# The sums of squares of an RMS norm, added over the partitions as two exact parts in fp32r products

## The chip, the cores and the metric

The kernel runs on one core of one Trainium2 chip. The metric is the device time of one launch in microseconds, taken as the median of three runs. A core has a matrix engine (PE, which loads a stationary operand and streams a moving one through it, the result landing in PSUM), a vector engine (DVE), a scalar engine (ACT), GpSimd (POOL) and SyncE (SP, which here issues nearly all the loads). Each engine takes its own instructions strictly in the order in which they were written into the program; between engines they wait for semaphores.

## The reference

A decoder trunk of two layers on 512 tokens of 1024 features, all in float32. Each sub-layer is wrapped in two RMS norms, and it is these norms that the change touches:

```python
def rms_norm(x, g):
    xf = x.astype(jnp.float32)
    y = xf * lax.rsqrt(jnp.mean(xf * xf, axis=-1, keepdims=True) + EPS)
    return (y * g.astype(jnp.float32)).astype(x.dtype)

f = swiglu(rms_norm(x, g[0]), w_ffn_gate[layer, 0], w_ffn_up[layer, 0], w_ffn_down[layer, 0])
x = x + 0.5 * rms_norm(f, g[1])
h = rms_norm(x, g[2])
# layer 0: m = short_conv_mixer(h, ...); layer 1: m = diff_attention(h, k, v, ...)
x = x + rms_norm(m, g[3])
f = swiglu(rms_norm(x, g[4]), ...)
x = x + 0.5 * rms_norm(f, g[5])
```

There are six sub-layers in a row: FFN, convolution, FFN (layer 0), FFN, attention, FFN (layer 1). So there are five boundaries between sub-layers, and at each of them the post-norm of one sub-layer is followed by the pre-norm of the next.

## The kernel before

Features lie on the 128 partitions (eight tiles `k` of 128), tokens on the free axis. Every large product is made in float32 accuracy from fp32r products: an operand is split into a rounded part `hi` (a cast, on ACT) and the exact rest `lo` (a subtraction, on DVE), and three products hi·hi, hi·lo and lo·hi are accumulated in one PSUM bank (`products`, lines 141 to 147). Weights come in units of 128x1024 over SP's queue into one of two `raw` buffers, and are split by a cast on ACT (`whi`, line 126) and a subtraction on DVE (`wlo`, line 127); seven split units are kept.

At a boundary (`closing`, line 254) the tokens are taken in two halves of 256 columns. `rms(t)` finishes the last tiles of the sub-layer's result `f` for one half, adds up the squares of its eight tiles in two accumulators (`facc0`, `facc1`, even and odd tiles, on DVE, line 190), and `total_of` (line 192) adds those up over the partitions: a PE product with the constant matrix `halves[D]` (all entries -0.5/1024), whose result `tot` stands in PSUM. `inv_rms` (line 169) turns it into 1/rms: ACT `n_y` (line 176), ACT `n_q` (line 178), DVE `n_q` (line 179), DVE `r` (line 180). `post` then scales `f`, adds it to the residual `x` and makes the `h_hi` and `h_lo` of the next sub-layer. The sequence is:

1. `rms(one)`, then `post` of the first half;
2. `rms(two)`, while the first half's `h` is made;
3. the head of the next sub-layer for the first half: PE products of `h` into PSUM banks `acc`;
4. `rest(one)`: squares of the new `x` of the first half, in `xacc0` and `xacc1`, their total, and the pre-norm factor `r2`;
5. the head's gate, which reads the `acc` banks, scales them by `r2` (lines 408 and 410; in the convolution lines 506 to 513) and so sets the banks free for the next PE products; `post` of the second half runs in between;
6. `rest(two)`.

There are six PSUM banks for such sums, and two small ones for `tot`.

Before the change `total_of` has two forms. With `merge` (the first half of `rms` and the second half of `rest`) DVE adds the two accumulators and one float32 product follows; without it (second half of `rms`, first half of `rest`) two float32 products are accumulated. There are 22 totals: ten in `rms` and twelve in `rest` (two of these before the first sub-layer), 11 of each form.

The order of the work on each engine isn't written out by hand. A scheduler decides it from its own costs when the program is built, so an edit in one helper can move other instructions.

Of the kernel before, what the change touches and what calls it, by code (L numbers as in the profile page):

```python
# [10 lines left out]
F32R = mybir.dt.float32r  # L11
BF16 = mybir.dt.bfloat16
AF = mybir.ActivationFunctionType
ALU = mybir.AluOpType
# [3 lines left out]
P = 128  # L18
D = 1024
S = 512  # L20
# [16 lines left out]
TEMPS = 4  # L37
HALF_TEMPS = 6
RAW = 2
WARM = 9  # L40
LAMBDA_INIT = 0.8 - 0.6 * math.exp(-0.3 * 1)
MASKED = -3.0e38
# [3 lines left out]
def yoco_kernel(ctx: ExitStack, tc, i, out):  # L46
    nc = tc.nc

    const = ctx.enter_context(tc.tile_pool(name="const", bufs=1))
    xpool = ctx.enter_context(tc.tile_pool(name="xpool", bufs=1))  # L50
    apool = ctx.enter_context(tc.tile_pool(name="apool", bufs=5 * NK))
    wsp = ctx.enter_context(tc.tile_pool(name="wsp", bufs=WUNITS))
    wraw = ctx.enter_context(tc.tile_pool(name="wraw", bufs=RAW))
    mpool = ctx.enter_context(tc.tile_pool(name="mpool", bufs=1))
    tpool = ctx.enter_context(tc.tile_pool(name="tpool", bufs=1))
    small = ctx.enter_context(tc.tile_pool(name="small", bufs=4))
    rpool = ctx.enter_context(tc.tile_pool(name="rpool", bufs=1))

    def slot(dtype, name):
        return apool.tile([P, S], dtype, tag="a", name=name)  # L60
# [7 lines left out]
    def temp(n=S, name="t"):  # L68
        if n <= S // 2:
            return tpool.tile([P, S // 2], F32, tag="th", name=name, bufs=HALF_TEMPS)[:, :n]  # L70
        return tpool.tile([P, S], F32, tag="t", name=name, bufs=TEMPS)[:, :n]
# [9 lines left out]
    halves = {}  # L81
    for n in (D, 2 * HD):
        halves[n] = const.tile([P, P], F32, name=f"half{n}")
        nc.vector.memset(halves[n], -0.5 / n)
    eps = const.tile([P, 1], F32, name="eps")
    nc.vector.memset(eps, EPS)
    gn = const.tile([P, 12, NK], F32, name="gn")
# [20 lines left out]
    warm = pst.tile([P, S], F32, tag="st", name="warm")  # L108
    for _ in range(WARM):
        nc.tensor.matmul(warm[:, :P], halves[D], halves[D], start=True, stop=True)  # L110
# [23 lines left out]
    def split(dst_hi, dst_lo, src, on_act=True):  # L134
        if on_act:
            nc.scalar.copy(dst_hi, src)  # L136
        else:
            nc.vector.tensor_copy(dst_hi, src)
        nc.vector.tensor_tensor(dst_lo, src, dst_hi.bitcast(F32), op=ALU.subtract)  # L139
# [29 lines left out]
    def inv_rms(total, dst, n, by_log=False):  # L169

        y = temp(n, "n_y")
        if by_log:
            nc.scalar.activation(y, total, AF.Ln, bias=eps, scale=-2.0)
            nc.scalar.activation(y, y, AF.Exp, scale=-0.5)
        else:
            nc.scalar.activation(y, total, AF.Abs_reciprocal_sqrt, bias=eps, scale=-2.0)
        q = temp(n, "n_q")
        nc.scalar.square(q, y)
        nc.vector.scalar_tensor_tensor(q, total, -0.5 * EPS, q, op0=ALU.add, op1=ALU.mult)
        nc.vector.scalar_tensor_tensor(dst, q, 1.5, y, op0=ALU.add, op1=ALU.mult)  # L180

    def squares_of(accs, src, m):

        acc = accs[m % 2]
        if m < 2:
            nc.scalar.square(acc, src)
        else:
            sq = temp(src.shape[-1], "sq")
            nc.scalar.square(sq, src)
            nc.vector.tensor_tensor(acc, acc, sq, op=ALU.add)  # L190

    def total_of(accs, n, merge):
        tot = pst.tile([P, S], F32, tag="st", name="tot")[:, :n]
        if merge:
            nc.vector.tensor_tensor(accs[1], accs[0], accs[1], op=ALU.add)
            nc.tensor.matmul(tot, halves[D], accs[1], start=True, stop=True)
            return tot
        for j, acc in enumerate(accs):
            nc.tensor.matmul(tot, halves[D], acc, start=j == 0, stop=j == 1)
        return tot  # L200

    def new_h():
# [2 lines left out]
    class Prenorm:  # L205
# [22 lines left out]
        def rest(self, t):  # L228
            a, b = t
            accs = [rpool.tile([P, S // 2], F32, tag=z, name=z) for z in ("xacc0", "xacc1")]  # L230
            for k in range(NK):
                squares_of(accs, x[:, k, a:b], k)
            inv_rms(total_of(accs, b - a, a > 0), self.r2[:, a:b], b - a)

    def post(f, r1, c, t, after, ks=range(NK)):

        a, b = t
        for k in ks:
            d = temp(b - a, "d")
            nc.vector.scalar_tensor_tensor(d, f[k][:, a:b], c[:, k : k + 1], r1, op0=ALU.mult, op1=ALU.mult)  # L240
            nc.vector.tensor_tensor(x[:, k, a:b], x[:, k, a:b], d, op=ALU.add)  # L241
            after.hi(k, t)
            if k > 0:
                after.lo(k - 1, t)
        if k == NK - 1:
            after.lo(k, t)
# [3 lines left out]
    def run(steps):  # L250
        for _ in steps:
            pass

    def closing(groups, c, after, then, step=2):

        f = [slot(F32, "f") if p is None else p for p in groups.parts]
        faccs = [rpool.tile([P, S], F32, tag=z, name=z) for z in ("facc0", "facc1")]

        def finish(ms, t):
            a, b = t
            for m, acc in zip(ms, groups(ms, t)):
                if groups.parts[m] is None:
                    nc.scalar.copy(f[m][:, a:b], acc)
                else:
                    nc.vector.tensor_tensor(f[m][:, a:b], f[m][:, a:b], acc, op=ALU.add)
                squares_of([z[:, a:b] for z in faccs], f[m][:, a:b], m)

        def rms(t):  # L270
            a, b = t
            for m in range(NK - TAIL, NK):
                finish([m], t)
            r1 = temp(b - a, "r1")
            inv_rms(total_of([z[:, a:b] for z in faccs], b - a, a == 0), r1, b - a)
            return r1

        for m in range(0, NK - TAIL, step):
            finish(range(m, m + step), FULL)
        one, two = HALVES  # L280
        post(f, rms(one), c, one, after)
        r1 = rms(two)
        ahead = then(one)
        next(ahead, None)
        after.rest(one)
        post(f, r1, c, two, after, range(POST_FIRST))
        next(ahead, None)
        post(f, r1, c, two, after, range(POST_FIRST, NK))
        run(ahead)
        after.rest(two)  # L290
        run(then(two))
# [548 lines left out]
```

## Time and profile before

| what | value |
| --- | --- |
| three runs, median (lowest to highest) | 1916.57 us (1916.27 to 1917.65) |
| the profiled execution's own time | 1915.81 us |
| its span, from the first to the last instruction | 1914.1 us |
| mean granted PE clock | 0.999 |
| PE, DVE and ACT busy | 99%, 52%, 39% of the span |

In the listings a PE product of 256 columns takes 0.28 us from start to end, but the next one starts after 0.11 to 0.12 us; what a product costs is read from start to start. A float32 product shows as two records.

### The profile page before, as it was taken

What the parts mean: (1) busy time and instruction counts of PE and PEld (TensorE: products, weight loads), DVE (VectorE), ACT (ScalarE), POOL (GpSimd) and SP (SyncE); (2) the same over time, 40 slices, a digit from 0 to 9 for tenths busy, and PEclk for the clock granted to TensorE, in tenths of its full rate; (3) what the DMA queues carried; (4) which work ended last, traced back from release to release, by engine and by line L of the source; (5) the groups of instructions that cost most, each with busy time, mean ns of one, the idle gap of its engine ahead of it and who ended that gap; (6) DMA issues with size and microseconds to landing.
All of it is one profiled execution on the core that took longest, in us unless ns stands there. A gap on an engine that the chain in (4) does not pass through costs nothing.

```text
span 1914.1 us, 24278 instructions
## 1 busy us (share of the span) xinstructions
PE 1896.1 (99%) x9780; PEld 1601.2 (84%) x9780; DVE 993.0 (52%) x1671; ACT 738.8 (39%) x1248; POOL 1.1 (0%) x8
## 2 busy tenths in 40 slices
PE   9999999999999999999999999999999999999998
PEld 8888888988898888888988888899866898888886
DVE  7423434574566334344862443457389594234345
ACT  7322222453354322222633222335289673332132
POOL 0000000000000000000000000000000000000000
PEclk9999999999999999999999999999999999999999
DMA  4432323233323323332233332323211224233331
GB/s 168 120 101 91 106 88 102 74 94 94 112 76 104 106 87 101 91 108 89 66 114 100 103 100 95 90 87 94 72 34 59 74 67 132 78 99 100 98 89 65
DMA packets 53375, 178.45 MB, mean 93 GB/s; under 512 B 6288, under 2 KB 9488, under 8 KB 53264
## 3 DMA queue, kind: packets, MB, share of 16 engines
q1 hardware_dynamic: 52400, 175.94, 29.5%
q8 instruction: 77, 1.26, 0.3%
q10 hardware_dynamic: 864, 0.97, 0.2%
q14 instruction: 34, 0.28, 0.1%
HBM read 174.79 MB, written 2.10 MB: 92 GB/s over the span
## 4 chain that ended last, share of the span: by engine, by line
PE 87%; DVE 8%; ACT 3%; issue 1%; DMA 1%; SPq 0%; DVEq 0%; ACTq 0%
PE acc L146 25%; PE acc L147 25%; PE acc L145 25%; PE d_acc L358 2%; PE d_acc L356 2%; PE d_acc L357 2%; DVE d L240 1%; DVE h_lo L219 1%; DVE x L241 1%; DVE wlo L127 1%; PE v_acc L604 1%; PE v_acc L605 1%; PE v_acc L606 1%; ACT e L647 1%; DVE top L642 1%
## 5 line engine op out<-in xcount | busy, mean ns | idle before, releaser
L145 PE MATMUL acc<-h_hi,whi 128*128 128x512 f32 (+1 forms) x1952 | 696.3, 358 | 2.3 <-ACT whi L126 1.5
L146 PE MATMUL acc<-h_lo,whi 128*128 128x512 f32 (+1 forms) x1952 | 696.3, 357 | 0.2
L147 PE MATMUL acc<-h_hi,wlo 128*128 128x512 f32 (+1 forms) x1952 | 695.4, 357 | 0.8 <-DVE wlo L127 0.8
L126 ACT CAST whi<-raw 128x1024 fp32r<-128x1024 f32 (+2 forms) x336 | 334.5, 1019 | 869.3 <-PE acc L146 731.1
L127 DVE TENSOR_TENSOR wlo<-raw,whi 128x1024 fp32r<-128x1024 f32 (+2 forms) x336 | 396.5, 1182 | 237.8 <-ACT whi L126 236.7
L145 PEld LDWEIGHTS acc<-h_hi,whi 128*128 128x128 f32 x1952 | 366.4, 188 | 57.5 <-ACT whi L126 2.0
L147 PEld LDWEIGHTS acc<-h_hi,wlo 128*128 128x128 f32 x1952 | 366.7, 188 | 55.2 <-DVE wlo L127 1.0
L146 PEld LDWEIGHTS acc<-h_lo,whi 128*128 128x128 f32 x1952 | 367.3, 188 | 54.4 <-DVE h_lo L219 0.8
L408 DVE TENSOR_TENSOR gs<-acc,r 128x512 f32<-128x512 f32 (+1 forms) x100 | 62.6, 626 | 446.9 <-PE acc L147 446.7
L146 PE MATMUL acc<-act_lo,whi 128*128 128x512 f32 (+1 forms) x624 | 223.3, 358 | 0.0
L145 PE MATMUL acc<-act_hi,whi 128*128 128x512 f32 (+1 forms) x624 | 222.7, 357 | 0.0
L147 PE MATMUL acc<-act_hi,wlo 128*128 128x512 f32 (+1 forms) x624 | 222.7, 357 | 0.0
L146 PEld LDWEIGHTS acc<-act_lo,whi 128*128 128x128 f32 x624 | 117.6, 189 | 18.4
L145 PEld LDWEIGHTS acc<-act_hi,whi 128*128 128x128 f32 x624 | 117.2, 188 | 18.0
L147 PEld LDWEIGHTS acc<-act_hi,wlo 128*128 128x128 f32 x624 | 117.2, 188 | 17.8
L136 ACT CAST act_hi<-us 128x512 fp32r<-128x512 f32 (+1 forms) x100 | 56.5, 568 | 64.2 <-DVE us L412 64.2
L356 PE MATMUL d_acc<-whi,act_hi 128*128 128x512 f32 x176 | 68.4, 389 | 0.0
L357 PE MATMUL d_acc<-whi,act_lo 128*128 128x512 f32 x176 | 68.3, 389 | 0.0
L358 PE MATMUL d_acc<-wlo,act_hi 128*128 128x512 f32 x176 | 68.3, 389 | 0.0
L410 DVE TENSOR_TENSOR us<-acc,r 128x512 f32<-128x512 f32 (+1 forms) x100 | 62.6, 626 | 0.0
L139 DVE TENSOR_TENSOR act_lo<-us,act_hi 128x512 fp32r<-128x512 f32 (+1 forms) x100 | 61.8, 621 | 0.7 <-ACT act_hi L136 0.7
L412 DVE TENSOR_TENSOR us<-us,gs 128x512 f32<-128x512 f32 (+1 forms) x100 | 61.7, 621 | 0.3
(156 smaller groups left out, 1647.6 us busy)
## 6 DMA issues: line engine op xcount, KB each, us to landing
raw<-in_wg SPq DMA_DIRECT2D x85, 512.0 KB, 3.7
raw<-in_wu SPq DMA_DIRECT2D x85, 512.0 KB, 3.4
raw<-in_wd SPq DMA_DIRECT2D x48, 448.0 KB, 3.4
raw<-in_wd SPq DMA_DIRECT2D x24, 512.0 KB, 3.8
raw<-in_wci SPq DMA_DIRECT2D x24, 512.0 KB, 3.5
raw<-in_wdt SPq DMA_DIRECT2D x22, 512.0 KB, 3.7
raw<-in_wco SPq DMA_DIRECT2D x8, 512.0 KB, 3.6
raw<-in_wq SPq DMA_DIRECT2D x8, 512.0 KB, 3.5
```

The costliest lines, as they stand in the source:

```text
L126: nc.scalar.copy(hi[:, z], raw[:, z])
L127: nc.vector.tensor_tensor(lo[:, z], raw[:, z], hi.bitcast(F32)[:, z], op=ALU.subtract)
L139: nc.vector.tensor_tensor(dst_lo, src, dst_hi.bitcast(F32), op=ALU.subtract)
L145: nc.tensor.matmul(acc, wh, ah, start=first and j == 0, stop=False)
L146: nc.tensor.matmul(acc, wh, al, start=False, stop=False)
L147: nc.tensor.matmul(acc, wl, ah, start=False, stop=last and j == n - 1)
L356: nc.tensor.matmul(acc, ah, wh, start=k == 0, stop=False)
L357: nc.tensor.matmul(acc, al, wh, start=False, stop=False)
L358: nc.tensor.matmul(acc, ah, wl, start=False, stop=k == m1 - m0 - 1)
L408: nc.vector.tensor_tensor(gs, g, r2[:, p:q], op=ALU.mult)
L410: nc.vector.tensor_tensor(us, up, r2[:, p:q], op=ALU.mult)
L412: nc.vector.tensor_tensor(us, us, gs, op=ALU.mult)
```

## The change

`total_of` loses its `merge` argument. Both accumulators are now split like any other operand, into `acc_hi` (ACT cast) and `acc_lo` (DVE subtraction), and four fp32r products with an fp32r copy of the constant matrix, `half_r`, are accumulated. The four new tiles and `half_r` need room, and the space reserved for descriptors of software-made DMA is set to 512 bytes; no DMA of the kernel is issued from POOL.

```diff
+SCRATCH = 512
...
+    half_r = const.tile([P, P], F32R, name="half_r")
+    nc.vector.tensor_copy(half_r, halves[D])
...
-    def total_of(accs, n, merge):
+    def total_of(accs, n):
+
         tot = pst.tile([P, S], F32, tag="st", name="tot")[:, :n]
-        if merge:
-            nc.vector.tensor_tensor(accs[1], accs[0], accs[1], op=ALU.add)
-            nc.tensor.matmul(tot, halves[D], accs[1], start=True, stop=True)
-            return tot
         for j, acc in enumerate(accs):
-            nc.tensor.matmul(tot, halves[D], acc, start=j == 0, stop=j == 1)
+            hi, lo = (rpool.tile([P, S // 2], F32R, tag=f"acc{z}{j}", name=f"acc_{z}")[:, :n] for z in ("hi", "lo"))
+            split(hi, lo, acc)
+            nc.tensor.matmul(tot, half_r, hi, start=j == 0, stop=False)
+            nc.tensor.matmul(tot, half_r, lo, start=False, stop=j == 1)
         return tot
...
-            inv_rms(total_of(accs, b - a, a > 0), self.r2[:, a:b], b - a)
+            inv_rms(total_of(accs, b - a), self.r2[:, a:b], b - a)
...
-            inv_rms(total_of([z[:, a:b] for z in faccs], b - a, a == 0), r1, b - a)
+            inv_rms(total_of([z[:, a:b] for z in faccs], b - a), r1, b - a)
...
-    nc = bacc.Bacc("TRN2", target_bir_lowering=False, num_devices=1)
+    nc = bacc.Bacc("TRN2", target_bir_lowering=False, num_devices=1, dynamic_dma_scratch_size=SCRATCH)
```

`split` (line 134) is the helper shown in its old place: a cast on ACT, then a subtraction on DVE. Lines after the first insertion have a number that is three higher in the changed kernel, and lines after line 197 of `total_of` likewise.

How the scheduler placed the new instructions is seen at three places. First PE, at the third boundary (second FFN of layer 0 to first FFN of layer 1), where the second half's total of `f` is made while the head's products run. `acc_…<-h_…,w…` are the head's products, `tot_…` the total. Before:

```order
L146 MATMUL acc_7417<-h_lo_5072,whi_7391 128x256
L147 MATMUL acc_7417<-h_hi_5071,wlo_7392 128x256
L199 MATMUL tot_7363<-facc0_6918,half1024_90 128x256
L199 MATMUL tot_7363<-facc1_6919,half1024_90 128x256
L145 MATMUL acc_7414<-h_hi_5073,whi_7373 128x256
```

and now, where the first of the four products (`tot_7475<-acc_hi_7476`) stands eleven rows above the first row shown with `acc_lo`:

```order
L148 MATMUL acc_7536<-h_hi_5177,whi_7495 128x256
L149 MATMUL acc_7536<-h_lo_5178,whi_7495 128x256
L202 MATMUL tot_7475<-acc_lo_7477,half_r_94 128x256
L201 MATMUL tot_7475<-acc_hi_7482,half_r_94 128x256
L150 MATMUL acc_7536<-h_hi_5177,wlo_7496 128x256
L202 MATMUL tot_7475<-acc_lo_7483,half_r_94 128x256
L148 MATMUL acc_7537<-h_hi_5177,whi_7501 128x256
```

The last product of this total has moved 15 head products later; the head's products themselves kept their order.

Second DVE at the same place: `facc` are the accumulators of the squares, `wlo` a weight unit's exact rest, `n_q` and `r1` the steps of `inv_rms`. Before:

```order
L190 TENSOR_TENSOR facc0_6918<-facc0_6918,sq_7330 128x256
L190 TENSOR_TENSOR facc1_6919<-facc1_6919,sq_7359 128x256
L127 TENSOR_TENSOR wlo_7907<-raw_7905,whi_7906 128x1024
L179 SCALAR_TENSOR_TENSOR n_q_7368<-tot_7363,n_q_7368 128x256
L180 SCALAR_TENSOR_TENSOR r1_7362<-n_q_7368,n_y_7366 128x256
```

and now:

```order
L193 TENSOR_TENSOR facc0_7020<-facc0_7020,sq_7442 128x256
L193 TENSOR_TENSOR facc1_7021<-facc1_7021,sq_7471 128x256
L130 TENSOR_TENSOR wlo_8049<-raw_8047,whi_8048 128x1024
L142 TENSOR_TENSOR acc_lo_7477<-facc0_7020,acc_hi_7476 128x256
L142 TENSOR_TENSOR acc_lo_7483<-facc1_7021,acc_hi_7482 128x256
L182 SCALAR_TENSOR_TENSOR n_q_7490<-tot_7475,n_q_7490 128x256
L183 SCALAR_TENSOR_TENSOR r1_7474<-n_q_7490,n_y_7488 128x256
```

The two new subtractions stand behind the `wlo`. Later at the same boundary, for `rest(one)`, the two subtractions stand right behind the six additions to `xacc`, with nothing in between.

Third DVE at the fifth boundary (attention to the last FFN), at `rest(one)`. Before:

```order
L190 TENSOR_TENSOR xacc0_13234<-xacc0_13234,sq_13250 128x256
L190 TENSOR_TENSOR xacc1_13235<-xacc1_13235,sq_13253 128x256
L127 TENSOR_TENSOR wlo_13124<-raw_13122,whi_13123 128x1024
L127 TENSOR_TENSOR wlo_13590<-raw_13588,whi_13589 128x1024
L240 SCALAR_TENSOR_TENSOR d_13265<-f_12699,gn_96,r1_13082 128x256
```

and now:

```order
L130 TENSOR_TENSOR wlo_13326<-raw_13324,whi_13325 128x1024
L193 TENSOR_TENSOR xacc0_13436<-xacc0_13436,sq_13452 128x256
L193 TENSOR_TENSOR xacc1_13437<-xacc1_13437,sq_13455 128x256
L130 TENSOR_TENSOR wlo_13812<-raw_13810,whi_13811 128x1024
L142 TENSOR_TENSOR acc_lo_13460<-xacc0_13436,acc_hi_13459 128x256
L142 TENSOR_TENSOR acc_lo_13466<-xacc1_13437,acc_hi_13465 128x256
L243 SCALAR_TENSOR_TENSOR d_13477<-f_12881,gn_98,r1_13274 128x256
```

Here the total's subtractions stand behind a second `wlo`, and the last two additions behind the first. At the second boundary (convolution to FFN) the same rows stand in the same order.

## The prediction

> **What bounds the kernel now.** The page first, for who is busy:
>
> ```profile
> span 1914.1 us, 24278 instructions
> PE 1896.1 (99%) x9780; PEld 1601.2 (84%) x9780; DVE 993.0 (52%) x1671; ACT 738.8 (39%) x1248; POOL 1.1 (0%) x8
> ```
>
> PE is busy nearly always, so work taken from PE looks like time won. Next the groups of PE instructions, for what is to be taken away:
>
> ```profile
> L199 PE MATMUL tot<-xacc,half 128*128 128x256 f32 x24 | 6.5, 392 | 0.2
> L199 PE MATMUL tot<-facc,half 128*128 128x256 f32 x20 | 5.7, 405 | 1.0 <-DVE facc L190 1.0
> L196 PE MATMUL tot<-xacc,half 128*128 128x256 f32 x12 | 4.2, 429 | 1.0 <-DVE xacc L195 1.0
> L196 PE MATMUL tot<-facc,half 128*128 128x256 f32 x10 | 3.5, 431 | 0.1
> ```
>
> That is 66 records, two for each of 33 float32 products: 11 totals with two products (L199), 11 with one (L196). What one costs is read where nothing waits, in PE's timeline at the start (start, duration):
>
> ```profile
> 20.87 0.28 PE L147 MATMUL acc<-h_hi,wlo 128*128 128x256 f32 x1
> 20.99 1.03 PE L199 MATMUL tot<-xacc,half 128*128 128x256 f32 x4
> 21.66 0.47 PE L145 MATMUL acc<-h_hi,whi 128*128 128x256 f32 x1
> 21.98 0.28 PE L146 MATMUL acc<-h_lo,whi 128*128 128x256 f32 x1
> 22.10 0.28 PE L147 MATMUL acc<-h_hi,wlo 128*128 128x256 f32 x1
> ```
>
> fp32r products start every 0.12 us. From 20.99 to 22.10 lie 1.11 us, of which two head products take 0.23, so the four float32 records take 0.88 us: 0.22 each, 0.44 a product.
>
> The third view decides: who sets the pace at a boundary between sub-layers. PE, ACT and DVE at the third boundary:
>
> ```profile
> 928.46 1.13 PE L199 MATMUL tot<-facc,half 128*128 128x256 f32 x4 [0.19 <-DVE facc L190]
> 933.20 1.13 PE L199 MATMUL tot<-xacc,half 128*128 128x256 f32 x4
> 938.73 0.28 PE L147 MATMUL acc<-h_hi,wlo 128*128 128x256 f32 x1
> 939.15 0.36 PE L145 MATMUL acc<-h_hi,whi 128*128 128x256 f32 x1 [0.15 <-DVE gs L408]
> ...
> 929.62 0.47 ACT L176 ACTIVATE n_y<-tot,eps 128x256 f32<-128x256 f32 x1 [2.24 <-PE tot L199]
> 934.37 0.48 ACT L176 ACTIVATE n_y<-tot,eps 128x256 f32<-128x256 f32 x1 [1.83 <-PE tot L199]
> ...
> 926.84 1.22 DVE L127 TENSOR_TENSOR wlo<-raw,whi 128x1024 fp32r<-128x1024 f32 x1
> 927.98 0.76 DVE L190 TENSOR_TENSOR facc<-facc,sq 128x256 f32<-128x256 f32 x2
> 928.65 1.22 DVE L127 TENSOR_TENSOR wlo<-raw,whi 128x1024 fp32r<-128x1024 f32 x1
> 930.58 0.42 DVE L179 SCALAR_TENSOR_TENSOR n_q<-tot,n_q 128x256 f32<-128x256 f32 x1 [0.71 <-ACT n_q L178]
> 931.38 2.10 DVE L190 TENSOR_TENSOR xacc<-xacc,sq 128x256 f32<-128x256 f32 x6
> 935.33 0.43 DVE L179 SCALAR_TENSOR_TENSOR n_q<-tot,n_q 128x256 f32<-128x256 f32 x1 [1.06 <-ACT n_q L178]
> 938.59 0.41 DVE L408 TENSOR_TENSOR gs<-acc,r 128x256 f32<-128x256 f32 x1
> ```
>
> PE's product at 939.15 needs a PSUM bank that the gate at 938.59 to 939.00 has just read; after 938.73 it would have been due at 938.85, so PE waits 0.3 us. What led to the gate is one chain: `facc` (ends 928.74), total, `n_y` 929.62, DVE's `n_q` and `r`, the six `xacc` additions (DVE takes them only after `r`), the second total, `n_y` 934.37, `n_q`, the gate. **Here the chain decides, not PE's work.** The other boundaries, PE again:
>
> ```profile
> 395.18 0.28 PE L147 MATMUL acc<-h_hi,wlo 128*128 128x256 f32 x1
> 395.92 0.96 PE L145 MATMUL acc<-h_hi,whi 128*128 128x256 f32 x3 [0.47 <-ACT h_hi L214]
> ...
> 573.62 0.55 PE L145 MATMUL acc<-h_hi,whi 128*128 128x256 f32 x2
> 574.00 0.28 PE L146 MATMUL acc<-h_lo,whi 128*128 128x256 f32 x1
> ...
> 1304.84 0.28 PE L147 MATMUL acc<-h_hi,wlo 128*128 128x256 f32 x1
> 1305.12 0.36 PE L145 MATMUL acc<-h_hi,whi 128*128 128x256 f32 x1
> ...
> 1558.36 0.71 PE L145 MATMUL acc<-h_hi,whi 128*128 128x256 f32 x2
> 1558.91 0.28 PE L146 MATMUL acc<-h_lo,whi 128*128 128x256 f32 x1
> ```
>
> At the first boundary 0.74 us lie between two starts, at the fourth 0.28 instead of 0.12, at the second and the fifth two products take 0.38 and 0.55 instead of 0.23. All five wait at this place, the second least.
>
> **PE's own work.** Removed: 33 x 0.44 = 14.5 us. Added: 88 fp32r products at the 0.12 of the rows above, 10.6 us. Per double total that is 0.88 - 0.48 = -0.4 us, per single one about 0. If PE set the time everywhere, the sum would be -3.9 us.
>
> [...]
>
> **The chain at the third boundary.** The casts and subtractions exist already for other tiles of this shape, so their price is measured:
>
> ```profile
> L136 ACT CAST act_hi<-us 128x256 fp32r<-128x256 f32 x24 | 9.3, 404 | 2.4 <-DVE us L412 2.4
> L139 DVE TENSOR_TENSOR act_lo<-us,act_hi 128x256 fp32r<-128x256 f32 x24 | 9.7, 418 | 0.0
> ```
>
> First total (second half of `f`). The new order puts both subtractions behind the `wlo` of 928.65. A `wlo` holds DVE for 1.14 us (926.84 to 927.98), so DVE is free at 929.79; two subtractions, 0.34 apart (six `xacc` in 2.10), end at 930.55. The casts, done by 929.2, are hidden under the `wlo`. The last product: 0.06 us hop (`facc0` ends 928.40, the total starts 928.46), 0.28 for the product, 0.04 to ACT: `n_y` at 930.9 instead of 929.62, **+1.3 us**.
>
> Second total (`rest(one)`): the additions end at 933.48 and `n_y` starts at 934.37, 0.89 later. Now follow a cast of 0.40, a subtraction of 0.42, the last product of 0.28 and four hops, in all 0.16: 1.26 us, **+0.37**.
>
> Together the gate comes 1.67 us later, and so does the PE product at 939.15. What PE saves in its two double totals before it only lengthens its wait there, because the chain starts from the last `f` tiles, which PE makes before either total. Around it: the first total of the boundary gains or loses nothing (0.44 plus a wait before; 0.48 plus a wait now), the one after the gate loses its wait for the merge (L195, whose `xacc` rows waited 1.0 in all), -0.1. So **+1.55 us** at the third boundary. The same order of rows stands at the first and the fourth, so 3 x 1.55 = **+4.65**.
>
> **Second and fifth boundary.** There the total of `rest(one)` had slack:
>
> ```profile
> 1546.57 2.09 DVE L190 TENSOR_TENSOR xacc<-xacc,sq 128x256 f32<-128x256 f32 x6
> 1551.95 1.23 DVE L127 TENSOR_TENSOR wlo<-raw,whi 128x1024 fp32r<-128x1024 f32 x1 [1.40 <-ACT whi L126]
> 1551.70 1.02 PE L199 MATMUL tot<-xacc,half 128*128 128x256 f32 x4
> 1552.76 0.47 ACT L176 ACTIVATE n_y<-tot,eps 128x256 f32<-128x256 f32 x1 [0.84 <-PE tot L199]
> ...
> 565.37 1.23 DVE L127 TENSOR_TENSOR wlo<-raw,whi 128x1024 fp32r<-128x1024 f32 x1 [1.06 <-ACT whi L126]
> 566.96 1.02 PE L199 MATMUL tot<-xacc,half 128*128 128x256 f32 x4
> ```
>
> The additions were done 3.0 us before the total at the fifth boundary. This slack takes up the first total's delay. But now the subtractions stand behind the second `wlo`, which waits for a weight transfer: 1551.95 + 1.14 + 0.34 + 0.42 = 1553.85, plus hops and product 0.38 = 1554.2 instead of 1552.76, +1.45; less about 0.25 around it, **+1.2**. At the second boundary the same `wlo` comes 1.6 us before PE's total instead of 0.25 after: 565.37 + 1.14 + 0.76 = 567.27 lies before the old total's end (566.96 + 0.88), so nothing is late there, and PE's saving of 0.8 us in two double totals is partly kept: **-0.3**. At the start, one double and one single total: **-0.3**.
>
> Sum: 4.65 + 1.2 - 0.3 - 0.3 = **+5.2 us**. Against the profiled execution's 1915.8 that is 1921.0; the median of the runs lies 0.76 above it, so **1921.8 us**. The `half_r` copy at the start (128 columns on DVE, far below the 0.42 of 256) lies before the first weights, and the DMA reserve touches no queue in use (the page counts none from POOL): both at nothing; uncovered, the copy costs at most 0.4.
>
> Bounds. Were the first stretch absorbed by DVE's idle 0.71 and 1.06 us, only 0.37 of it would remain at three boundaries. Upwards, each of the 22 totals has up to three places to wait where it had one or two; a refill after a wait costs 0.10 (four records last 1.13 after a wait, 1.03 without), and the waits here were 0.1 to 0.3.
>
> **The rivals.** *PE decides* (0.08): the scheduler moved the totals later so that nothing waits, the gates keep pace, and PE's -3.9 us and some waits are won: 1911 to 1913 us. For it: 99% busy. Against it: the products at 939.15 and 395.92, which start when the gate lets them.
>
> *Half a chain* (0.20): the first stretch vanishes in DVE's idle gaps and only the second counts: 3 x (0.37 - 0.1) + 0.5 - 0.6 = +0.7, so 1917.3 us, no change. Against it: both gaps are waits for `n_q`, which comes from the same chain and moves along.
>
> *A wait at each part* (0.10): the lo products wait too, 0.2 us and the refill each at two in three places, some 4.4 us on top: 1926 us. Against it: PE's order puts them up to 15 products, 1.7 us, later.
>
> *The change doesn't do what it says*: the fp32r copy would still run as float32, in two records. All other fp32r products show one record and 0.12 us; not counted.
>
> My forecast (0.62) is the lengthened chain. This kernel can't be told from no change within 0.2%, 3.8 us. The forecast's own spread of about 1.5 us puts a ninth of it under that line: slower 0.55 + 0.10 = 0.65, same 0.07 + 0.20 = 0.27, faster 0.08. The range goes from 1916.6, which holds most of the half chain, to 1925.0, which holds the forecast's upper end and the lighter cases of a wait at each part; left out are PE decides and about as much above.
>
> **What would show it.** `tot` in 88 records of about 0.12 us from start to start; the gate's PE product at the first, third and fourth boundary waiting some 2 us instead of 0.2 to 0.6 (the 1.67 and PE's saving); 2.2 us from the end of `facc` to `n_y` at the third boundary instead of 0.88; a `wlo` in front of `acc_lo`. Wrong, if PE has no gap before the products that follow the gate, or if `acc_lo` starts before the `wlo`.

## The result

The changed kernel is slower: 1926.67 us (median of six runs, 1925.54 to 1929.18) against 1916.42 us (six runs, 1915.71 to 1917.65). The ratio is 1.0054, 95% interval 1.0043 to 1.0064, so 10.2 us. The direction was predicted, the size was not: 1921.8 us was forecast, and the range ended at 1925.0. Three single runs in the rounds further below took 2351 to 3830 us, one of them of the kernel before; every ratio leaves them out.

The page of the changed kernel gives PE as busy as before, at 99%:

```profile
span 1923.7 us, 24399 instructions
PE 1897.2 (99%) x9802; PEld 1604.2 (83%) x9802; DVE 1004.0 (52%) x1705; ACT 754.0 (39%) x1292; POOL 1.1 (0%) x8
```

The totals are what was forecast: 44 products with `acc_hi` and 44 with `acc_lo`, one record each (the groups of the instructions that touch `tot`; durations in ns, least, median and largest):

```profile
L201 PE MATMUL tot<-acc_hi,half_r x44: 279/284/391, 21.7 to 1581.3; 128*128 128x256 f32 x44
L202 PE MATMUL tot<-acc_lo,half_r x44: 278/283/391, 21.8 to 1581.5; 128*128 128x256 f32 x44
```

Where the 10 us lie is found by matching PE's products of the two traces one by one (the totals left out), and taking start after minus start before. That lead grows at five places:

| place | forecast | measured, us |
| --- | --- | --- |
| start, up to 50 us | -0.3 | +0.6 |
| first boundary | +1.55 | +2.0 |
| second | -0.3 | +0.1 |
| third | +1.55 | +3.4 |
| fourth | +1.55 | +2.2 |
| fifth | +1.2 | +1.9 |

Between these places the lead stays the same within 0.3 us; it is 9.7 us at the end, and the two profiles' spans differ by 9.6. The start is the least certain row, because it differs from profile to profile (see below). Now the third boundary, the place that the forecast worked out. The timeline of the changed kernel, DVE first, then ACT, then PE:

```profile
930.72 0.76 DVE L193 TENSOR_TENSOR facc<-facc,sq 128x256 f32<-128x256 f32 x2
931.39 1.22 DVE L130 TENSOR_TENSOR wlo<-raw,whi 128x1024 fp32r<-128x1024 f32 x1
932.53 0.75 DVE L142 TENSOR_TENSOR acc_lo<-facc,acc_hi 128x256 fp32r<-128x256 f32 x2
935.54 2.10 DVE L193 TENSOR_TENSOR xacc<-xacc,sq 128x256 f32<-128x256 f32 x6
937.77 0.76 DVE L142 TENSOR_TENSOR acc_lo<-xacc,acc_hi 128x256 fp32r<-128x256 f32 x2
943.33 0.42 DVE L411 TENSOR_TENSOR gs<-acc,r 128x256 f32<-128x256 f32 x1
...
931.17 0.74 ACT L139 CAST acc_hi<-facc 128x256 fp32r<-128x256 f32 x2 [1.05 <-DVE facc L193]
933.78 0.48 ACT L179 ACTIVATE n_y<-tot,eps 128x256 f32<-128x256 f32 x1 [1.86 <-PE tot L202]
939.11 0.47 ACT L179 ACTIVATE n_y<-tot,eps 128x256 f32<-128x256 f32 x1 [1.03 <-PE tot L202]
...
940.90 0.28 PE L150 MATMUL acc<-h_hi,wlo 128*128 128x256 f32 x1
943.89 0.55 PE L148 MATMUL acc<-h_hi,whi 128*128 128x256 f32 x1 [2.71 <-DVE gs L411]
944.24 0.41 PE L149 MATMUL acc<-h_lo,whi 128*128 128x256 f32 x1
944.46 0.41 PE L150 MATMUL acc<-h_hi,wlo 128*128 128x256 f32 x1
944.67 0.41 PE L148 MATMUL acc<-h_hi,whi 128*128 128x256 f32 x1
```

From the end of `facc` (931.48) to `n_y` (933.78) pass 2.30 us; before it was 0.88. The casts are done at 931.91, but the subtractions start at 932.53, when the `wlo` lets DVE go. From `n_y` to `n_y` pass 5.33 us (before 4.75), from the second `n_y` to the gate's `gs` 4.22 as before. So the chain is 1.42 + 0.58 = 2.0 us longer, and PE waits 2.71 us for the gate, where the row of before (939.15) had 0.15.

The last PE rows show what the forecast did not have: after the wait, products start 0.21 us apart instead of 0.115. The windows view of the changed kernel says why (columns: window, its length, busy time and count of PE, PEld, DVE, ACT, POOL, then the granted PE clock, DMA share, GB/s):

```profile
940.00:943.60 3.60, 1.18 (x11) 0.98 (x9) 3.54 (x10) 2.08 (x7) 0.00 (x0) 1.00 0.00 0
943.60:947.10 3.50, 3.21 (x15) 3.24 (x16) 3.50 (x11) 3.08 (x6) 0.00 (x0) 0.51 0.00 0
947.10:950.00 2.90, 2.90 (x28) 2.90 (x28) 2.90 (x9) 1.02 (x2) 0.00 (x0) 1.00 0.02 6
```

For 3.4 us the granted clock is half (the windows round it to 0.51), and 15 products fit in where some 30 would. They lose about 15 x 0.097 = 1.4 us, and that is what the third boundary has above the others. There is a second such spell at 15.2 to 18.6 us in this profile; in that of before there is none but at the very end, when PE has nothing left to do.

### The profile page after: what moved, and what is told of

It is laid out like the page before. It is cut to its first block, busy times and chain, and to the rows that moved or that the text cites. A ratio compares the mean times of both kernels' runs of the same rounds, so it can differ in the third digit from the quotient of the medians.

```text
span 1923.7 us, 24399 instructions
## 1 busy us (share of the span) xinstructions
PE 1897.2 (99%) x9802; PEld 1604.2 (83%) x9802; DVE 1004.0 (52%) x1705; ACT 754.0 (39%) x1292; POOL 1.1 (0%) x8
## 4 chain that ended last, share of the span: by engine, by line
PE 88%; DVE 7%; ACT 3%; DMA 1%; issue 1%; SPq 0%; DVEq 0%; ACTq 0%
PE acc L148 26%; PE acc L149 26%; PE acc L150 26%; PE d_acc L360 2%; PE d_acc L359 2%; PE d_acc L361 2%; DVE d L243 1%; DVE wlo L130 1%; DVE h_lo L222 1%; DVE x L244 1%; ACT whi L129 1%; PE v_acc L607 1%; PE v_acc L608 1%; PE v_acc L609 1%; ACT e L650 1%; DVE top L645 1%
```

## The experiments

My theory after the result: the longer chain of `rms(two)` and `rest(one)` makes the gate late and PE idle (some 8 us), and the idle time brings on spells of half clock (the rest). The rivals: a wait at every part of every total; the reserve or the new tiles cost something by themselves; the spells are mere chance.

**The reserve alone.**

```
+SCRATCH = 512
-    nc = bacc.Bacc("TRN2", target_bir_lowering=False, num_devices=1)
+    nc = bacc.Bacc("TRN2", target_bir_lowering=False, num_devices=1, dynamic_dma_scratch_size=SCRATCH)
```

> The kernel before with the 512-byte descriptor reserve alone. Lengthened chain (my theory): the reserve carries no traffic, so 1916.4 us, ratio 1.000. Rival 'the reserve costs': if a part of the 10.2 us comes from the space itself, 1918 us or more.

Measured 1917.24 us against 1917.99 us for before on the same chip, ratio 0.9997 (0.9987 to 1.0006). The reserve costs nothing. Note that the kernel before had 1916.4 us above and 1918.0 us here: its runs go with their mean granted clock. Of its 30 runs here the eight at 0.999 have a median of 1916.2 us, the eighteen at 0.998 1918.2, the four at 0.997 1919.4. One spell of 3.4 us at half clock takes 1.7 / 1917 = 0.0009 off the mean, so 0.001 of clock is about one spell and about 1.6 us. By this reckoning some runs of the kernel before have such spells too; its one profile shows none between the start and the end.

**One place at a time.** `total_of` keeps its two old forms beside the new one, and an added last argument says where the new one is taken. For the second half of `rms` alone the calls read

```
-            inv_rms(total_of(accs, b - a, a > 0), self.r2[:, a:b], b - a)
+            inv_rms(total_of(accs, b - a, a > 0, False), self.r2[:, a:b], b - a)
...
-            inv_rms(total_of([z[:, a:b] for z in faccs], b - a, a == 0), r1, b - a)
+            inv_rms(total_of([z[:, a:b] for z in faccs], b - a, a == 0, a > 0), r1, b - a)
```

for the first half of `rest` alone the two are `a == 0` and `False`, for the merged places `a > 0` and `a == 0`. DVE's order at the boundaries changes nowhere but at the place chosen, save some weight units at the second and the fifth and, in the kernel with the merged places, some instructions right behind `rest(two)`.

> The four-product total at the second half of rms alone; the other three places as before. Lengthened chain: the end of facc to n_y grew by 1.42 us at the third boundary of the changed kernel; the same at the first, third and fourth gives +4.3 us, to which a spell of half clock of 1.4 us may come: 1920.5 to 1922.5 us, with PE waiting 1.5 to 2 us at the gate of these boundaries. Rival 'a wait at each part' (a cost that goes by the number of totals, 5 of 22 of 10.2 us): +2.3 us, 1918.7 us. Rival 'PE decides': 5 totals of -0.4 us, 1914.4 us.

> The four-product total at the first half of rest alone. Lengthened chain: n_y to n_y grew by 0.58 us; at three boundaries +1.7 us, at the fifth, where the subtractions may stand behind a wlo, up to +1.6 us, and the gain at the start about -0.2: 1918 to 1919.5 us. Rival 'a wait at each part' (6 of 22 totals): +2.8 us, 1919.2 us, but then with waits at tot and not at the gate. Rival 'PE decides': 1914.0 us.

> The four-product total at the two merged places alone (first half of rms, second half of rest; 11 of the 22 totals). Lengthened chain: neither is on the chain to the gate, and PE has 0.48 instead of 0.44 us: 1916 to 1917 us, ratio 1.000. Rival 'a wait at each part': 11 of 22 totals, +5.1 us, 1921.5 us.

| kernel | median, us | ratio to before (95%) | lead won at boundary 1 / 2 / 3 / 4 / 5, us |
| --- | --- | --- | --- |
| second half of `rms` | 1921.83 | 1.0020 (1.0010 to 1.0029) | 1.3 / -0.1 / 1.2 / 1.5 / 0.4 |
| first half of `rest` | 1918.43 | 1.0000 (0.9990 to 1.0010) | 0.45 / 0.0 / 0.4 / 0.7 / -0.2 |
| merged places | 1917.90 | 1.0001 (0.9992 to 1.0010) | 0.0 / 0.7 / 0.35 / 0.0 / 0.4 |
| the change | 1926.67 | 1.0054 (1.0043 to 1.0064) | 2.0 / 0.1 / 3.4 / 2.2 / 1.9 |

The third boundary with the second half of `rms` alone:

```profile
928.98 0.75 DVE L193 TENSOR_TENSOR facc<-facc,sq 128x256 f32<-128x256 f32 x2
932.03 0.48 ACT L179 ACTIVATE n_y<-tot,eps 128x256 f32<-128x256 f32 x1 [1.86 <-PE tot L203]
936.78 0.47 ACT L179 ACTIVATE n_y<-tot,eps 128x256 f32<-128x256 f32 x1 [1.83 <-PE tot L210]
941.56 0.36 PE L148 MATMUL acc<-h_hi,whi 128*128 128x256 f32 x1 [1.76 <-DVE gs L419]
```

and with the first half of `rest` alone:

```profile
929.93 0.75 DVE L193 TENSOR_TENSOR facc<-facc,sq 128x256 f32<-128x256 f32 x2
931.56 0.48 ACT L179 ACTIVATE n_y<-tot,eps 128x256 f32<-128x256 f32 x1 [2.24 <-PE tot L210]
936.90 0.48 ACT L179 ACTIVATE n_y<-tot,eps 128x256 f32<-128x256 f32 x1 [1.04 <-PE tot L203]
941.69 0.35 PE L148 MATMUL acc<-h_hi,whi 128*128 128x256 f32 x1 [1.02 <-DVE gs L419]
```

Each place lengthens its own stretch and leaves the other as it was: 2.30 and 4.75 us in the first kernel, 0.88 and 5.34 in the second. At the first, third and fourth boundary the terms add up to the change's within 0.25 us (the third without its 1.4 us of half clock). Eleven of the 22 totals, the merged ones, cost nothing that can be measured, so the cost does not go by the number of totals. At the second and the fifth boundary they do not add up: at the fifth 0.4 - 0.2 + 0.4 alone, 1.9 together. The traces show what differs at the fifth. With `rest` alone, the scheduler puts its two subtractions behind one late `wlo`; in the changed kernel they stand behind a second one, which waits for its cast:

```profile
1560.71 1.22 DVE L130 TENSOR_TENSOR wlo<-raw,whi 128x1024 fp32r<-128x1024 f32 x1 [0.26 <-ACT whi L129]
1561.85 0.75 DVE L142 TENSOR_TENSOR acc_lo<-xacc,acc_hi 128x256 fp32r<-128x256 f32 x2
```

From the end of `facc` to the second `n_y` pass 9.17 us before, 8.84 with `rms` alone, 9.10 with `rest` alone and 10.92 in the changed kernel. No run moves that `wlo`, so its share is read from the traces and not tested. In time, `rest` alone lies within its interval of nothing, so its +1.3 us rests on the profile alone.

**The `wlo` behind the subtractions.** The changed kernel, with one ordering edge that moves a `wlo` at three boundaries: the first weight unit of the next body takes its `wlo` after the last `acc_lo` of `rms(two)`. (The last piece below stands first in the file.)

```
+        last_lo[0] = nc.vector.tensor_tensor(dst_lo, src, dst_hi.bitcast(F32), op=ALU.subtract)
...
         r1 = rms(two)
+        guard[:] = last_lo
...
+            if guard and past == 0:
+                with tc.issue_after(guard.pop().ins):
+                    nc.vector.tensor_tensor(lo[:, z], raw[:, z], hi.bitcast(F32)[:, z], op=ALU.subtract)
+            else:
...
```

> The changed kernel, with the one wlo that stood in front of the two acc_lo of the second half of rms put behind them (first, third and fourth boundary; no other instruction moves on DVE). Theory (the subtractions are late because they queue behind that wlo): the end of facc to n_y falls from 2.30 us to about 1.3 (cast 0.41, subtraction 0.42, product 0.28, hops), so -1.0 us at each of three boundaries, and the spell of half clock at the third boundary may go with the shorter idle time (-1.4): 1922 to 1924 us, against 1926.7 for the change. Rival 'the wlo only fills a time in which acc_lo would wait for its casts on ACT anyway': the end of facc to n_y stays above 2 us and the time at 1926.7.

DVE and ACT at its third boundary:

```profile
929.06 0.74 DVE L199 TENSOR_TENSOR facc<-facc,sq 128x256 f32<-128x256 f32 x2
929.94 0.76 DVE L148 TENSOR_TENSOR acc_lo<-facc,acc_hi 128x256 fp32r<-128x256 f32 x2
930.62 1.22 DVE L134 TENSOR_TENSOR wlo<-raw,whi 128x1024 fp32r<-128x1024 f32 x1
931.20 0.47 ACT L185 ACTIVATE n_y<-tot,eps 128x256 f32<-128x256 f32 x1 [0.96 <-PE tot L208]
```

`n_y` comes 1.40 us after `facc`'s end instead of 2.30, and the same at the first and the fourth boundary; at the second and the fifth, where another `wlo` stands in front and did not move, it stays at 2.3. The median is 1922.82 us, ratio 1.0030 (1.0018 to 1.0041) against 1.0054: as expected. One instruction in front of the subtractions made some 0.9 us at each of three boundaries, and no work was taken away. The ratios lie 4.6 us apart, more than these 2.7: the runs' mean clock is 0.9977 against the change's 0.9968, which by the reckoning above would be some 1.4 us. The wait at the gate of the third boundary is still 1.81 us, and this profile has a spell of half clock at the third and at the fourth boundary, so the expected end of the spells did not come.

**PE kept busy through the wait.**

```
             inv_rms(total_of(accs, b - a), self.r2[:, a:b], b - a)
+            if a == 0 and self.gi in (6, 8):
+                warm = pst.tile([P, S], F32, tag="st", name="warm")[:, : b - a]
+                for _ in range(6):
+                    nc.tensor.matmul(warm, halves[D], self.r2[:, a:b], start=True, stop=True)
```

> The changed kernel with six float32 products added behind r2 of the first half at the third and fourth boundary, whose result nobody reads; they last 2.64 us and stand just in front of the product that waits 2.87 us for the gate. Theory (the idle time of PE brings on the half clock that follows it): no half clock at these two boundaries, the other products there start every 0.12 us, -1.4 us where the spell was: about 1925 us and a mean granted clock of 0.998. Rival 'the spells come by chance, whatever PE does there': a spell is as likely as before, 1926.7 us. If the products don't fit into the idle time, up to +5 us.

```profile
942.28 2.86 PE L240 MATMUL warm<-r,half 128*128 128x256 f32 x12
944.96 0.36 PE L148 MATMUL acc<-h_hi,whi 128*128 128x256 f32 x1
945.15 0.28 PE L149 MATMUL acc<-h_lo,whi 128*128 128x256 f32 x1
```

In its profile there is no half clock at either boundary, the products start 0.12 us apart from the second on, and the third boundary costs 2.25 us instead of 3.4. But the median is 1926.44 us, ratio 1.0048 (1.0033 to 1.0063), which is not told apart from the change, and the fourth boundary came out 0.8 us dearer. That is not the filling products' doing: 17 us ahead of them a cast waits for a weight transfer,

```profile
1293.73 1.05 ACT L129 CAST whi<-raw 128x1024 fp32r<-128x1024 f32 x1 [0.99 <-DMA raw<-in_wq]
```

and the chain is 0.7 us later from there on, while PE's product follows the gate by 0.56 us as in the change. One profile without a spell can be chance. By its time this run is inconclusive on the spells.

**The gate two tiles earlier, and two tiles later.** Two kernels, `POST_FIRST = 2` and `POST_FIRST = 6` in place of 4. The first shortens PE's wait, the second doubles it.

> The changed kernel with POST_FIRST 2 instead of 4: the gate's first gs then stands on DVE behind one x and one h_lo after r2, instead of six instructions of post. r2 is there at 941.16 in the changed kernel, the gs at 943.33. Theory (PE waits for the gate, and the gate for what stands ahead of it on DVE): the gate comes about 1.2 us earlier at three boundaries, -3.6 us and perhaps the spell, 1922 to 1924 us, unless the post of the second half, now later, makes its head wait. Rival 'the wait is not for the gate's place but for the total's PE work': 1926.7 us.

> The changed kernel with POST_FIRST 6 instead of 4: on DVE the first gs of the gate now stands behind six more instructions of post (some 2.2 us) than in the changed kernel. This doubles the suspected cause. Theory (the gate's place sets when PE goes on, and PE's idle time brings on half clock): PE waits about 4.5 to 5 us instead of 2.9 at the gate of the third and fourth boundary, and about 4 at the first, +5 to +6 us in all; the profile shows a spell of half clock of 3.4 us behind most of these waits, and the runs' mean clock falls to 0.996 or lower: 1931 to 1936 us. Rival 'the spells come by chance, whatever PE does there': +5 to +6 us alone, with a mean clock as in the changed kernel, about 0.997, and no spell, or one, at the three gates.

The third boundary with 2:

```profile
940.62 0.47 ACT L179 ACTIVATE n_y<-tot,eps 128x256 f32<-128x256 f32 x1 [1.03 <-PE tot L202]
943.31 0.42 DVE L411 TENSOR_TENSOR gs<-acc,r 128x256 f32<-128x256 f32 x1
```

`gs` follows 2.69 us behind `n_y` at the third boundary instead of 4.22, and PE's idle time there falls from 2.8 to 1.2 us; but 1.0 us comes back some 3 to 5 us later, where two products wait for the second half's `h_hi` (0.48) and `h_lo` (0.52): its `post` is now later, as the expectation's "unless" says. Its profile has a spell at the first boundary and none at the third. 1924.70 us, ratio 1.0041 (1.0026 to 1.0055): about half of what I expected, with an interval that overlaps the change's.

With 6 the kernel takes 1945.23 us, ratio 1.0146 (1.0131 to 1.0162), 19 us more than the change and far more than expected. The waits of PE for the gate (total, count, longest):

```profile
PE acc L148 <- DVE gs L411: 11.7, 3, 5.7
PE acc L148 <- DVE q L565: 5.6, 1, 5.6
PE acc L148 <- ACT cs L498: 4.6, 1, 4.6
```

and the windows behind the third and the fourth gate:

```profile
953.00:960.00 7.00, 5.03 (x24) 5.07 (x25) 6.81 (x20) 4.71 (x9) 0.00 (x0) 0.51 0.00 0
1325.00:1332.00 7.00, 4.20 (x20) 4.23 (x21) 7.00 (x21) 3.37 (x9) 0.00 (x0) 0.51 0.01 2
```

Every boundary has a spell, 3.4 or 6.8 us long, and the runs' mean clock is 0.990 to 0.992. The rival that the spells have nothing to do with what PE does is out: longer idle times bring them on. How much of the 19 us is clock and how much waiting was not taken apart. (The waits grew by 3.0 us, not 2.2, and the second and fifth boundary, where I expected nothing, lost too; hence the size.)

**The start.** In the changed kernel the two totals ahead of the first sub-layer get their old form back (`self.gi > 0` chooses the new one).

> The changed kernel, with the two totals ahead of the first sub-layer made as before (two float32 products; merge and one). In the profile of the change a spell of half clock lies at 15 to 18.6 us, in that of before none does. Theory (the start costs what its own totals cost): their chain and the spell go, -0.6 to -1.5 us: 1925 to 1926 us, and no half clock before 30 us. Rival 'the spell at the start comes by chance': half clock there as in the change, time 1926.7 us.

1927.55 us, ratio 1.0056 (1.0039 to 1.0073): nothing is won. Its first stretch has half clock as the change has (the same window in the profiles of this kernel, of the change and of before):

```profile
14.00:20.00 6.00, 4.43 (x22) 4.23 (x23) 5.21 (x8) 5.99 (x11) 0.00 (x0) 0.72 1.06 385
```

```profile
14.00:20.00 6.00, 5.25 (x32) 5.25 (x33) 6.00 (x10) 5.57 (x12) 0.00 (x0) 0.72 1.00 362
```

```profile
14.00:20.00 6.00, 5.08 (x40) 4.85 (x41) 5.86 (x8) 6.00 (x13) 0.00 (x0) 1.00 1.07 382
```

So the totals of the start do not cause the spell there; my expectation was wrong. The kernel with the `wlo` moved shows the other half: it has the new totals at the start and no spell there. PE has gaps in this stretch in every one of these kernels, and the lead at 50 us went from -0.5 to +2.8 us among them. What decides whether a spell falls there I have not found.

**No second parts.** The last addition writes an fp32r tile, which goes into the product as it is:

```
+            dst = acc
+            if m >= NK - 2:
+                j, n = m % 2, src.shape[-1]
+                dst = accs[j] = rpool.tile([P, S // 2], F32R, tag=f"acchi{j}", name="acc_r")[:, :n]
+            nc.vector.tensor_tensor(dst, acc, sq, op=ALU.add)
...
         for j, acc in enumerate(accs):
+            nc.tensor.matmul(tot, half_r, acc, start=j == 0, stop=j == 1)
```

> The change without its second parts: the last addition to each accumulator writes an fp32r tile, and two fp32r products with half_r make the total; no cast, no subtraction, no merge. This changes the computation: the sums of squares are rounded to fp32r before they are added over the partitions. Theory (the chain decides, and PE's savings are kept where the chain is no longer than before): per double total PE saves 0.64 us and the chain 0.4 us, per merged one 0.2 us and the addition's 0.36: of the full 9.2 us on PE some 4 to 7 are kept, 1909 to 1913 us. Rival 'a wait at each total, whatever its form': no change from before, 1916.4 us.

1910.52 us against 1917.05, ratio 0.9963 (0.9949 to 0.9976): faster than both kernels, as expected. The third boundary:

```profile
924.75 0.43 DVE L197 TENSOR_TENSOR acc_r<-facc,sq 128x256 fp32r<-128x256 f32 x1
925.65 0.48 ACT L179 ACTIVATE n_y<-tot,eps 128x256 f32<-128x256 f32 x1 [1.50 <-PE tot L203]
936.30 0.36 PE L148 MATMUL acc<-h_hi,whi 128*128 128x256 f32 x1 [0.90 <-DVE gs L413]
```

From the last addition's end (925.18) to `n_y` 0.47 us, less than the 0.88 of before. The lead falls by 1.9, 1.4, 1.0, 1.3 and 0.7 us at the five boundaries: here PE's savings are kept, since the chain is not longer. The price is accuracy, how much was not measured: the sums go into the product as fp32r alone, without their second parts.

## Why the prediction was half right

The way and the mechanism at the boundaries were right, the sum was not: +5.2 us forecast, 10.2 measured. The step that failed is the pricing of PE's wait. It was priced at its own length, with the clock put at nothing, and at the third boundary a spell of half clock added 1.4 us. The rest of the shortfall is in terms that were sized too small: 0.5 us at each of the first, third and fourth boundary, 0.7 at the fifth, and savings of 0.3 each at the second and at the start that did not come (0.4 and 0.9). No one term makes the whole miss.

- **The chain decides, not PE's work: right.** PE's 99% and its -3.9 us of own work told nothing; what PE saved went into longer waits. Only the kernel with `acc_r`, whose chain is shorter too, got faster.
- **First total, +1.3: right**, 1.42 measured, with the `wlo` in front of `acc_lo` as the order showed; putting it behind gave 0.9 back.
- **Second total, +0.37: too small**, 0.58 measured (5.33 - 4.75). I added the durations and four hops of 0.04. In the trace the last addition ends at 937.64, the second subtraction at 938.53 and `n_y` starts at 939.11: both steps of the split come in pairs, and the last product queues behind a head product on PE (0.58 us from the subtraction's end to `n_y`, where 0.28 and the hops were forecast).
- **Around it, -0.1: not found.** The three boundaries came to 2.0, 2.0 (without the spell) and 2.2 us instead of 1.55: 1.5 us in all.
- **Fifth boundary, +1.2: 1.9; second, -0.3: 0.1.** The subtractions behind the late `wlo` are there, and the slack took up the first total's delay nearly whole: that `wlo` starts 8.47 us after `facc`'s end, 8.36 before. What was too small is the step from the last subtraction (1562.60) to `n_y` (1563.16), 0.56 us instead of 0.38, and the 0.25 taken off "around it" did not come. And the 0.8 us that PE saves at the second was not kept; why, the runs do not show.
- **Start, -0.3: 0.6**, with a spell of half clock that the totals there do not cause. Among the profiles this row goes from -0.5 to +2.8, so one profile cannot size it.
- **Missing from the sum and from its bounds: the clock.** I priced PE's wait at its own length. In the changed kernel, PE idle for 2.7 us came back at half clock and lost 1.4 us more. The six runs of the change have mean clocks of 0.996 to 0.998 (mean 0.9968), the kernel before 0.997 to 0.999 (mean 0.9981 of the 30 runs above). At 1.6 us for 0.001 this is about 2 us of the 10.2, an estimate. It may be more: those 30 runs are of another round, the clocks of the six runs beside the change's are not on record, and their median of 1916.4 us goes with a clock near 0.999, which would make it 3.5 us. The page had a clock of 0.999 throughout, and I took it as given.

The rival "a wait at each part" names a time near the measured one, 1926 us, by another mechanism, and that one fell: that its number is near is luck. PE's waits in the changed kernel (total, count, longest):

```profile
PE acc L148 <- DVE gs L411: 3.3, 2, 2.7
PE acc L148 <- DVE q L565: 2.7, 1, 2.7
PE tot L201 <- ACT acc_hi L139: 2.4, 6, 0.9
PE acc L148 <- ACT cs L498: 1.7, 1, 1.7
PE tot L202 <- DVE acc_lo L142: 0.4, 1, 0.4
```

Before the gate PE waits 7.7 us in the three `acc` groups; at the totals 2.8 us, against 1.0 + 1.0 in the rows L196 and L199 of before, and the lo products (L202) waited once, 0.4 us. "Half a chain" fell with the 2.30 us, "PE decides" with the result. What was said to show the forecast right is there: 88 records, waits of 1.7 to 2.7 us at three gates ("some 2 us"), 2.30 us from `facc` to `n_y` ("2.2"), and the `wlo` in front.

## What to carry to other kernels

An edit that makes PE's work cheaper by adding steps on other engines must be priced by the chain that those steps lengthen, and by what stands in front of them on their engine: here one `wlo` at each of three boundaries made some 3 of the 10 us. A wait of PE did not always cost its own length only: of the 13 idle times of 1.7 to 2.9 us in the profiles here, five were followed by half clock, which made 1.4 us more at the third boundary. So a kernel whose PE already waits at a boundary should get a shorter chain before its PE work is shaved. If the accuracy allows it, letting the last addition write the rounded type gives the cheap product with no step added.

## What the runs showed of the hardware

All idle times of PE above 1 us behind the first 30 us, in the profiles of the twelve kernels shown or named here (start to start, less 0.16 us), and whether the granted clock fell to half near the restart:

| idle, us | times | followed by half clock |
| --- | --- | --- |
| 1.0 to 1.3 | 23 | 0 |
| 1.7 to 2.0 | 8 | 3 |
| 2.5 to 2.9 | 5 | 2 |
| 3.6 to 5.8 | 4 | 4 |

The spells last 3.41 us, or 6.83 for the three longest idle times. In the profile of the changed kernel the granted clock changes at 15.18, 18.60, 943.61, 947.02 and 1919.82 us, and these times lie whole numbers of 3.4133 us apart, within 0.005 us (1, 271, 1 and 285 of them).

Counted by stretch of this grid instead of by gap, the table gets clearer. Here is PE's idle time (the length less PE's busy time in the windows view) in each stretch of 3.41 us at full clock, between the start and the end of the twelve profiles:

| idle in the stretch, us | stretches | next stretch at half clock |
| --- | --- | --- |
| up to 1.6 | some 6600 | 0 |
| 1.69 to 1.94 | 8 | 4 |
| 2.40 to 3.41 | 5 | 5 |

So between the start and the end of these profiles no stretch with up to 1.6 us idle was followed by half clock, every one with 2.40 us or more was, and of the eight from 1.69 to 1.94 us four were. The start does not fit in: in the changed kernel the stretch from 11.77 to 15.18 us has 1.45 us idle (PE busy for 1.96 of 3.41 us), and half clock follows. The count does set apart the idle time of 2.8 us at the third boundary of the changed kernel, which half clock followed, and that of 2.8 us at the fourth, which it did not. The first row is the third boundary's stretch, with 2.43 us idle; the other two are the fourth's, where the gap falls across two stretches, 1.80 and 0.92 us:

```profile
940.20:943.61 3.41, 0.98 (x9) 0.78 (x7) 3.41 (x10) 2.06 (x6) 0.00 (x0) 1.00 0.00 0
1308.84:1312.25 3.41, 1.61 (x15) 1.41 (x13) 2.90 (x9) 1.96 (x6) 0.00 (x0) 1.00 0.00 0
1312.25:1315.66 3.41, 2.49 (x21) 2.52 (x22) 3.41 (x11) 1.02 (x2) 0.00 (x0) 1.00 0.02 5
```

What differs between these two waits is where they fall on the grid, and the grid does not stand alike in the two main profiles: counted back from a change of the clock in steps of 3.4133 us, its first point lies 1.53 us behind the span's start in the changed kernel (change at 15.18 us) and 2.86 us in the kernel before (its one change, at 1910.92 us).
